# Moving the conv branch product of a hybrid streaming-encoder block from behind the gates to between attention and the gates

## The chip, the cores and the metric

The kernel runs on one core of a Trainium2 chip. The metric is the device time of one execution in microseconds (us), and less is better. The engines are named as in the profile: PE (TensorE, matrix products), DVE (VectorE), ACT (ScalarE), POOL (GpSimd) and SP (SyncE, which here issues every DMA between the core's memory, SBUF, and the chip's main memory, in one queue, in order). Every engine runs its own instructions in order, and waits at an instruction until what it needs is there.

## The reference

One layer for a sequence of 1024 rows of 1024 numbers, in float32. Cut to what matters here:

```python
h = modulate(rms_norm(x, g_pre_mix), sh1, sc1)
proj = h @ w_in                      # -> bg, cg, u, q, k, v (512 each), ga, gb (1024 each)
y_conv = short_conv_branch(bg, cg, u, conv_w) @ w_proj_conv     # bg * conv3(cg * u), 512 -> 1024
o = stick_breaking_attention(q, k, v)                           # 8 heads of 64
y_attn = o @ w_proj_attn                                        # 512 -> 1024
merged = sigmoid(ga) * y_conv + sigmoid(gb) * y_attn
x = x + gt1 * rms_norm(merged @ w_out, g_post_mix)
h2 = modulate(rms_norm(x, g_pre_mlp), sh2, sc2)
x = x + gt2 * rms_norm(square(relu(h2 @ w_mlp_in)) @ w_mlp_out, g_post_mlp)
```

`mod = c @ w_ada + b_ada` gives `sh1` to `gt2`, six rows of 1024.

## The kernel before, in words

Every large product is made of three products of reduced-precision parts: each operand is split into a high part (an ACT cast) and a low part (a DVE subtraction of the high part), and PE adds high x high, high x low and low x high in a PSUM bank of 128x512 (there are 8 banks). Activations lie transposed, channels on the 128 partitions. `hT` (`hTh`, `hTl`) holds `h` in both parts.

The stages, in order of time in the program:

1. Norm, first modulation, `hT`, and the value rows of attention.
2. Attention, with PE's order written out by hand. Between its steps PE does the other projections of `h` (q, k, and bg, cg, u of the conv branch) as `fill`, in banks `mm` (L545). The conv branch's four products `y` (128x1024 each, tile `cy`) are stored in `y_d` (L627) as they are done. Some 86 projection matmuls are left when attention ends.
3. The gates, `proj[:, 3072:]` for `ga` and `gb`, 2048 columns in 8 pairs of 128. Each pair is one Strassen-Winograd product: 7 products in place of 8, in the order 1, 2, 6, 5, 7, 3, 4, each of 4 x 3 matmuls (L233). Its right factors come from `hT` and are the same for all pairs: 1, 2 and 3 are parts of `hT`, and 4 to 7 are made from sums of its quarters: DVE adds high and low parts again (`e`, 16 additions L93), makes 16 differences (L90), and ACT and DVE split 16 results into `gy4`, `gy6`, `gy7` and, in place, a part of `hT` (factor 5). Its left factors are 128x512 sums of `w_in` columns, split for each pair (tiles `t`). `done` evicts a result: a DVE sum (L843), the sigmoid on ACT (L844) and a store to `sg_d` (L846). Between the factors runs `modulation`: four products of `c` with a 1024-column part of `w_ada`, each as 8 multiply-adds on DVE (L144) into `acc`, over 8 loads of 512 KB into two buffers; `acc` is first cleared by POOL (L139), gets a part of `b_ada` by DMA (L140), and PE sums its partitions at the end (L865 in rounds 1 and 4, L153 in 2 and 3).
4. The conv branch: `y` is loaded from `y_d` (`yr`), split (`br`), and multiplied with `w_proj_conv`: 8 rows of 128 channels, 2 halves, 12 matmuls each, 192 in all. DVE multiplies each bank with the gate row loaded from `sg_d` (L951).
5. The attention branch, the same with `o` from `o_d` (`or`) and `w_proj_attn`: DVE multiplies with the gate (L976), adds the conv row (L93), and splits the sum into `mT` (`mTh`, `mTl`).
6. `mix_block`: `w_out`, the norm and the residual; then the MLP's two products.

Inside stages 1 and 2 the order on PE is the hand-written one. Elsewhere a scheduler orders the instructions of each engine by its own estimate of their times. Tiles come from pools: a tile that is opened where another pool lay waits until the old tiles there have been read.

Of the kernel before, what the change touches and what calls it, by code (L numbers as in the profile page):

```python
# [8 lines left out]
F32 = mybir.dt.float32  # L9
# [7 lines left out]
P = 128  # L17
# [13 lines left out]
def block_kernel(  # L31
# [40 lines left out]
    y_d = dram.tile([4, P, T], F32, name="y_d")  # L72
# [464 lines left out]
    psm = open_pool(psm_es, "psm", bufs=3, space=PSUM)  # L537
# [13 lines left out]
    with ExitStack() as es:  # L551
# [235 lines left out]


    ga0 = 3 * CW + 3 * NH * HD
    psg_es = ExitStack()  # L790
    with ExitStack() as es:
        gt = open_pool(es, "gt")
        gy = open_pool(es, "gy", side="right")
        yop = resident(hT)
# [3 lines left out]
        quads = []  # L798
        for k in range(4):
            q11, q12, q22, q21 = (gt.tile([P, HALF], F32, tag="e", name=nm("e"), bufs=8) for _ in range(4))  # L800
            quads.append([[q11, q12], [q21, q22]])
            for o, i in zip((q11, q12, q22, q21), (1, 5, 3, 2)):
                hi, lo = yop[i][k]
                add(o, f(hi), f(lo), nc.vector)
            for o, l, r in ((q11, q12, q11), (q12, q22, q12), (q22, q22, q11), (q21, q21, q22)):
                sub(o, l, r, nc.vector)
            for i in (6, 7, 4):
                split_t(quads, yop, i, k)
        for _ in fill:
            pass  # L810
        for k in range(4):
            split_t(quads, yop, 5, k)
        psm_es.close()
        psg = open_pool(psg_es, "psg", bufs=8, space=PSUM)

        MODS = (14, 2)
        calls = [0]

        def gate_factors(p):
            split_of = pair_factors(  # L820
                column_pair(w_in, ga0 + 2 * p * P),
                lambda: gt.tile([P, 4, P], F32, tag="s", name=nm("s"), bufs=4),
                lambda i: gt.tile([P, 4, P], F32R, tag="e", name=nm("t"), bufs=8)
                if p >= 2 and i in (7, 3, 4)
                else gt.tile([P, 4, P], F32R, tag="t", name=nm("t"), bufs=12),
            )
# [8 lines left out]
            return with_modulation  # L835

        def gate_products(p, xop):
            fo = out_pair()

            def done(r, half, ps, kept):  # L840
                o = fo[r][:, half, :]
                if kept is not None:
                    nc.vector.tensor_tensor(o, ps, kept, op=ALU.add)  # L843
                nc.scalar.activation(o, ps if kept is None else o, AF.Sigmoid)  # L844
                if (r, half) in ((0, 1), (1, 0)):
                    nc.sync.dma_start(sg_d[2 * p + r], flat(fo[r]))  # L846

            if p == KC - 1:
                for _ in mods:
                    pass  # L850
                load_y()
            return pair_products(psg, 4, xop, yop, keeper(fo), done)
# [27 lines left out]
        yq = []  # L880

        def load_y():
            for k, tag in zip(range(4), ("cu", "cy", "acc", "row")):
                t = cv.tile([P, T], F32, tag=tag, name=nm("yr"), bufs=1)
                nc.sync.dma_start(t, y_d[k])
                yq.append(t)

        pipeline(KC, gate_factors, gate_products)
# [4 lines left out]
    gp_es, br_es, cy_es = ExitStack(), ExitStack(), ExitStack()  # L893
    gp = open_pool(gp_es, "gp", bufs=16)
    ow = open_pool(br_es, "ow")
    cyp = open_pool(cy_es, "cyp", side="right")
# [4 lines left out]
    def branch_operand(pool, raw, engines):  # L901

        parts_of = []
        for k in range(4):
            hi, lo = (pool.tile([P, T], F32R, name=nm("br")) for _ in "hl")
            split(raw[k], hi, lo, engines[k])
            parts_of.append([(hi[:, h], lo[:, h]) for h in halves])
        return parts_of

    def branch_weight(w, p, eng):  # L910

        raw = raw_tile((P, 4, 2 * P))
        nc.sync.dma_start(
            raw, w[:, 2 * p * P : (2 * p + 2) * P].rearrange("(a p) n -> p a n", p=P)
        )
        hi, lo = raw_tile((P, 4, 2 * P), "wh"), raw_tile((P, 4, 2 * P), "wl")
        hi, lo = hi.bitcast(F32R), lo.bitcast(F32R)
        split(raw, hi, lo, eng)
        return hi, lo

    def branch(w, operand, m0, use, engines):

        ahead = branch_weight(w, 0, engines[0])
        for p in range(KC // 2):
            hi, lo = ahead
            if p + 1 < KC // 2:
                ahead = branch_weight(w, p + 1, engines[p + 1])
            for m in (2 * p, 2 * p + 1):
                sg = ow.tile([P, T], F32, tag="sg", name=nm("sg"), bufs=4)
                nc.sync.dma_start(sg, sg_d[m0 + m])  # L930
                s = slice((m % 2) * P, (m % 2 + 1) * P)
                for half in range(2):
                    ps = bank(psg, "s")
                    mm3(ps, [((hi[:, k, s], lo[:, k, s]), operand[k][half]) for k in range(4)])
                    use(m, half, ps, sg[:, halves[half]])


    OPERANDS = "vvvv vvvv vvvv vvvv"
    MERGED = "vvvvvvvvvvvvvvvv vvvvvvvvvvvvvvvv"
    branch_on, merged_on = on(OPERANDS), on(MERGED)  # L940
    yop = branch_operand(cyp, yq, branch_on[0])
    oq = []
    for k, tag in zip(range(4), ("cu", "cy", "acc", "row")):
        t = cv.tile([P, T], F32, tag=tag, name=nm("or"), bufs=1)
        nc.sync.dma_start(t, o_d[k])
        oq.append(t)
# [8 lines left out]
    cy_es.close()  # L955
# [17 lines left out]

    def merged(m, half, ps, sg):
        o, t = ow.tile([P, HALF], F32, tag="o", name=nm("o"), bufs=4), g1[m, half]
        nc.vector.tensor_tensor(o, ps, sg, op=ALU.mult)  # L976
# [15 lines left out]
    branch(w_proj_attn, oop, KC, merged, branch_on[3])  # L992
# [388 lines left out]
```

## Time and profile before

| | us |
|---|---|
| median of 3 runs | 1456.64 |
| lowest and highest | 1454.67, 1458.77 |
| the profiled execution | 1457.99 |
| its span in the profile | 1456.3 |

The profiled execution is 1.35 us longer than the median of the runs, and its time is 1.7 us longer than the span, which goes from the first to the last instruction. An engine's busy time is a share of the span; where PE, the busiest engine, waits, and for whom, is read from the views of the trace.

### The profile page before, as it was taken

The page shows a single profiled execution, that of the slowest core. Times are in us where ns is not written, and L with a number is a line of the kernel's source. Part 1 is how long each engine was busy: PE and PEld are TensorE (multiplying, and loading weights), DVE is VectorE, ACT ScalarE, POOL GpSimd, SP SyncE. Part 2 cuts the span into 40 slices and gives each one's busy share as a digit, 9 for nine tenths or more (in the row PEclk, how much of TensorE's full clock was granted, in tenths as well). Part 3 has the DMA queues.
Part 4 walks back from the last instruction along what each step waited for, and adds up shares of the span by engine and source line. Part 5 has one row for each costly group of instructions (what it writes and reads, how often), then busy time and mean ns, then how long its engine had stood idle before and what let it go on. Part 6 is the DMA issues. An engine that isn't in the chain of part 4 may idle for free.

```text
span 1456.3 us, 17855 instructions
## 1 busy us (share of the span) xinstructions
PE 1374.5 (94%) x6281; PEld 1123.7 (77%) x6281; DVE 1076.1 (74%) x1684; ACT 645.2 (44%) x1301; POOL 95.8 (7%) x187
## 2 busy tenths in 40 slices
PE   5899899999996999899999899999999899999996
PEld 4788777887884888678878688888888688888884
DVE  6728888887879777357635886665654998989998
ACT  5636656565533433333346643333322544434432
POOL 1002112212200000000011000000000000000001
PEclk9899999999998999999999899999999999999999
DMA  8501110111114567575432243322346425151224
GB/s 299 179 15 35 36 53 21 37 37 51 44 55 129 190 222 236 202 250 167 136 103 100 73 145 116 117 87 89 116 142 217 152 80 174 59 165 38 77 84 173
DMA packets 107566, 171.09 MB, mean 117 GB/s; under 512 B 7322, under 2 KB 66766, under 8 KB 107476
## 3 DMA queue, kind: packets, MB, share of 16 engines
q1 hardware_dynamic: 107476, 169.95, 35.5%
q8 instruction: 49, 0.80, 0.2%
q14 instruction: 41, 0.34, 0.1%
HBM read 132.16 MB, written 37.76 MB: 117 GB/s over the span
## 4 chain that ended last, share of the span: by engine, by line
PE 76%; DVE 14%; DMA 3%; ACT 3%; issue 3%; POOL 1%; SPq 0%; DVEq 0%; ACTq 0%; POOLq 0%
PE s L233 28%; PE s L1274 19%; PE mm L545 8%; PE s L120 4%; PE s L121 4%; PE s L122 4%; PE v L507 3%; DVE pt L688 2%; PE o L729 2%; DVE a L692 2%; PE tr L718 1%; DMA wa<-in_w_ada_dram 1%; DMA raw<-in_w_in_dram 1%; POOL a L684 1%; DVE tu L90 1%
## 5 line engine op out<-in xcount | busy, mean ns | idle before, releaser
L1274 PE MATMUL s<-y,y 128*128 128x512 f32 x984 | 236.8, 393 | 8.4 <-DVE ffacc L1284 3.9
L1274 PEld LDWEIGHTS s<-y,y 128*128 128x128 f32 x984 | 185.4, 189 | 50.5 <-DVE ffacc L1284 5.1
L545 PE MATMUL mm<-hTh,wh 128*128 128x512 f32 x320 | 129.1, 403 | 0.0
L545 PE MATMUL mm<-hTl,wh 128*128 128x512 f32 x320 | 125.5, 392 | 0.0
L545 PE MATMUL mm<-hTh,wl 128*128 128x512 f32 x320 | 125.5, 392 | 0.0
L103 ACT CAST y<-g 128x512 fp32r<-128x512 f32 x104 | 58.6, 620 | 128.0 <-PE s L1274 107.6
L233 PE MATMUL s<-hTh,t 128*128 128x512 f32 x256 | 83.9, 398 | 14.4 <-ACT hTh L103 14.3
L688 DVE TENSOR_TENSOR_SCAN pt<-pt,dmask 128x128 f32<-128x128 f32 (+3 forms) x64 | 87.1, 1365 | 8.5 <-ACT pt L681 8.1
L1284 DVE TENSOR_TENSOR ffacc<-s,ffacc 128x512 f32<-128x512 f32 x124 | 83.7, 691 | 8.9 <-PE s L1274 8.8
L233 PE MATMUL s<-mTh,g 128*128 128x512 f32 x256 | 86.2, 404 | 3.7 <-ACT mTh L103 3.7
L103 ACT CAST tu<-tr 128x512 fp32r<-128x512 f32 (+2 forms) x112 | 49.1, 439 | 78.2 <-PE tr L718 49.5
L131 POOL TENSOR_TENSOR rstd<-var,mhalf 128x1 f32<-128x1 f32 x32 | 23.1, 725 | 920.0 <-DVE var L128 919.9
L90 DVE TENSOR_TENSOR tu<-tr,tu 128x512 fp32r<-128x512 f32 (+2 forms) x112 | 55.1, 494 | 34.5 <-ACT tu L103 33.5
L233 PE MATMUL s<-mTh,h 128*128 128x512 f32 x240 | 79.6, 396 | 0.0
L1274 PE MATMUL s<-fr,fr 128*128 128x512 f32 x288 | 74.6, 392 | 0.0
L233 PE MATMUL s<-y,g 128*128 128x512 f32 x288 | 71.5, 391 | 0.0
L233 PE MATMUL s<-y,h 128*128 128x512 f32 x288 | 71.5, 391 | 0.0
L90 DVE TENSOR_TENSOR y<-g,y 128x512 fp32r<-128x512 f32 x104 | 67.9, 691 | 3.8 <-PE s L1274 2.0
L545 PEld LDWEIGHTS mm<-hTh,wl 128*128 128x128 f32 x320 | 60.2, 188 | 13.4
L233 PEld LDWEIGHTS s<-hTh,t 128*128 128x128 f32 x256 | 48.6, 190 | 25.9 <-ACT hTh L103 14.6
L545 PEld LDWEIGHTS mm<-hTl,wh 128*128 128x128 f32 x320 | 60.5, 189 | 8.9
L545 PEld LDWEIGHTS mm<-hTh,wh 128*128 128x128 f32 x320 | 60.4, 189 | 8.8
(258 smaller groups left out, 3138.3 us busy)
## 6 DMA issues: line engine op xcount, KB each, us to landing
raw<-in_w_in_dram SPq DMA_DIRECT2D x38, 512.0 KB, 3.8
wa<-in_w_ada_dram SPq DMA_DIRECT2D x32, 512.0 KB, 3.9
raw<-in_w_mlp_in_dram SPq DMA_DIRECT2D x32, 512.0 KB, 3.8
g<-in_w_mlp_out_dram SPq DMA_DIRECT2D x40, 256.0 KB, 3.7
g<-f_d SPq DMA_DIRECT2D x40, 256.0 KB, 3.5
sg<-sg_d SPq DMA_DIRECT2D x16, 512.0 KB, 3.5
f_d<-wl SPq DMA_DIRECT2D x16, 512.0 KB, 5.0
f_d<-wh SPq DMA_DIRECT2D x16, 512.0 KB, 2.6
```

What stands on the lines that cost most here:

```text
L90: eng.tensor_tensor(o, a, b, op=ALU.subtract)
L103: nc.scalar.copy(hi, src)
L120: nc.tensor.matmul(ps, lh, rh, start=i == 0, stop=False)
L121: nc.tensor.matmul(ps, lh, rl, start=False, stop=False)
L122: nc.tensor.matmul(ps, ll, rh, start=False, stop=i == n - 1)
L233: nc.tensor.matmul(ps, l, r, start=first and k == 0 and j == 0, stop=k == nk - 1 and j == 2, skip_group_check=True,)
L507: nc.tensor.matmul(vb[b], l, r, start=k == 0 and i == 0, stop=k == KC - 1 and i == 2, skip_group_check=True,)
L545: nc.tensor.matmul(ps, w[a][:, k, :], hT[b][:, k, s], start=k == 0 and i == 0, stop=k == KC - 1 and i == 2, skip_group_check=True,)
L688: nc.vector.tensor_tensor_scan(pt[:, 0:w][:, ::-1], pt[:, 0:w][:, ::-1], dmask[:, T - w : T][:, ::-1], 1.0, ALU.mult, ALU.max,)
L692: nc.vector.tensor_tensor(a[:, 0:w], a[:, 0:w], pt[:, 1 : w + 1], op=ALU.mult)
L1274: nc.tensor.matmul(ps, l[:, s], r, start=start and j == 0 and n == 0, stop=j == len(fs) - 1 and n == 2, skip_group_check=True,)
L1284: nc.vector.tensor_tensor(o, ps, o, op=ALU.add)
```

## The change

The conv branch product (stage 4) is taken from behind the gates and put between the last projection and the gates. `y` 0 to 2 are loaded back from `y_d`; `y` 3 is taken from SBUF. The result of the product, without a gate, goes by ACT copies (`rows`) to memory, `yc_d`. While it runs, the right factors of the gates are made in turns with it: `right_factors` is a generator with one step per DVE instruction or split, of which one is taken at every fourth projection step (`FILL_TURNS`) and two after each bank of the conv branch (`BANK_TURNS`). In this stretch the order on PE, DVE and ACT is the order of the code (`manual_schedule`). The first two left factors of the first gate pair are made in the same stretch, in weight buffers. When a conv row's gate is done, DVE multiplies it with the row loaded from `yc_d`, and `sg_d` holds the gated conv row. The attention branch then loads both: the other gate as before, and the gated conv rows as 16 halves. Stage 4 as such is gone; the operand of the attention branch is loaded where `load_y` stood (`load_o`).

The diff, cut to its core:

```diff
-    y_d = dram.tile([4, P, T], F32, name="y_d")
+    y_d = dram.tile([3, P, T], F32, name="y_d")
+    yc_d = dram.tile([KC, P, T], F32, name="yc_d")
...
-                nc.sync.dma_start(y_d[k, :, s], y[:, s])
+                if k < 3:
+                    nc.sync.dma_start(y_d[k, :, s], y[:, s])
...
+        def right_factors():
+            quads = []
+            for k in range(4):
+                q11, q12, q22, q21 = (eslot() for _ in range(4))
+                quads.append([[q11, q12], [q21, q22]])
+                for o, i in zip((q11, q12, q22, q21), (1, 5, 3, 2)):
+                    hi, lo = yop[i][k]
+                    add(o, f(hi), f(lo), nc.vector)
+                    yield
+                for o, l, r in ((q11, q12, q11), (q12, q22, q12), (q22, q22, q11), (q21, q21, q22)):
+                    sub(o, l, r, nc.vector)
+                    yield
+                for i in (6, 7, 4):
+                    split_t(quads, yop, i, k)
+                    yield
+                if k:
+                    split_t(quads, yop, 5, k - 1)
+                    yield
+            split_t(quads, yop, 5, 3)
+            yield
+
+        def conv_branch(raws, turns):
...
+            for n, _ in enumerate(fill):
+                if n in LEAD:
+                    what, k = LEAD[n]
+                    {"y": operand, "w": weight}[what](k)
+                elif n % 4 in FILL_TURNS:
+                    next(turns)
+            yield
+            weight(1)
+            operand(3)
...
+            banks = [(m, half) for m in range(KC) for half in range(2)]
+            held = {}
+            for n, (m, half) in enumerate(banks[:4] + banks):
...
+                ks = range(3) if n < 4 else range(3, 4) if n < 8 else range(4)
...
+                if n >= 4:
...
+                    nc.scalar.copy(rows[m][:, halves[half]], ps)
+                    if half:
+                        nc.sync.dma_start(yc_d[m], rows[m])
+                if n >= 4 and m % 2 == 0 and half == 0 and p + 2 < KC // 2:
+                    weight(p + 2)
+                if n == 17:
+                    gate_split.append(gate_factors(0))
+                    for i in (1, 2):
+                        gate_first[i] = gate_split[0](i)
+                for _ in range(BANK_TURNS):
+                    next(turns, None)
+            for _ in turns:
+                pass
...
+        LEAD = {1: ("y", 0), 3: ("y", 1), 5: ("y", 2), 18: ("w", 0)}
+        FILL_TURNS, BANK_TURNS = (0,), 2
...
+        with tc.manual_schedule(
+            engines={mybir.EngineType.PE, mybir.EngineType.DVE, mybir.EngineType.Activation}
+        ):
+            stages = conv_branch(raws, right_factors())
...
         def gate_products(p, xop):
             fo = out_pair()
+            yc = {}
+            if p < KC // 2:
+                for r in range(2):
+                    for half in range(2):
+                        yc[r, half] = eslot()
+                        nc.sync.dma_start(yc[r, half], yc_d[2 * p + r, :, halves[half]])
...
                 nc.scalar.activation(o, ps if kept is None else o, AF.Sigmoid)
+                if yc:
+                    nc.vector.tensor_tensor(o, o, yc[r, half], op=ALU.mult)
...
-        pipeline(KC, gate_factors, gate_products)
+        gt = open_pool(es, "gt")
+        pipeline(KC, gate_factors, gate_products, first=(gate_first, gate_split[0]))
...
-    yop = branch_operand(cyp, yq, branch_on[0])
...
-    def gated(m, half, ps, sg):
-        t = g1[m, half] = gslot()
-        nc.vector.tensor_tensor(t, ps, sg, op=ALU.mult)
-
-    branch(w_proj_conv, yop, 0, gated, branch_on[1])
-    oop = branch_operand(ow, oq, branch_on[2])
+    oop = branch_operand(oq, lambda: ow.tile([P, T], F32R, name=nm("br")), branch_on[2])
...
+    def gate_rows(m):
+        sg = ow.tile([P, T], F32, tag="sg", name=nm("sg"), bufs=4)
+        nc.sync.dma_start(sg, sg_d[KC + m])
+        for half in range(2):
+            t = g1[m, half] = gslot()
+            nc.sync.dma_start(t, sg_d[m, :, halves[half]])
+        return sg
```

What the change does to the instructions of an engine is seen in three places. In these rows the number behind a name is that of the buffer. The first place is PE at the end of the projections (`mm` banks). Before:

```order
L545 MATMUL mm_4093<-hTh,wh_3906 128x512
L545 MATMUL mm_4093<-hTl,wh_3906 128x512
L545 MATMUL mm_4093<-hTh,wl_3907 128x512
L233 MATMUL s_4174<-hTh,t_4136 128x512
L233 MATMUL s_4174<-hTl,t_4136 128x512
L233 MATMUL s_4174<-hTh,t_4137 128x512
```

In the changed kernel (`br`: the parts of `y`; `wh`, `wl`: the parts of `w_proj_conv`):

```order
L546 MATMUL mm_4060<-hTh,wh_3907 128x512
L546 MATMUL mm_4060<-hTl,wh_3907 128x512
L546 MATMUL mm_4060<-hTh,wl_3908 128x512
L903 MATMUL s_4102<-br_3963,wh_4042 128x512
L903 MATMUL s_4102<-br_3964,wh_4042 128x512
L903 MATMUL s_4102<-br_3963,wl_4043 128x512
```

The first product of the gates, on the whole right factor in `hT`, stood behind the projections; now the 192 matmuls of the conv branch stand there, and the gates behind them. PE has 6247 matmuls in both programs.

The second place is DVE where the gates begin. In the changed kernel (`s`: sums of left factors, `t`: their parts, `acc`: the modulation's sum):

```order
L91 TENSOR_TENSOR gy4l<-e_4313,gy4h 128x512
L94 TENSOR_TENSOR s_4437<-raw_4381,raw_4383 128x512
L91 TENSOR_TENSOR s_4438<-s_4437,raw_4381 128x512
L91 TENSOR_TENSOR s_4439<-raw_4381 128x512
L91 TENSOR_TENSOR hTl<-e_4194,hTh 128x512
L145 SCALAR_TENSOR_TENSOR acc_4651<-wa_4654,vcols,acc_4651 128x1024
L91 TENSOR_TENSOR s_4440<-raw_4383,s_4438 128x512
L91 TENSOR_TENSOR hTl<-e_4310,hTh 128x512
L91 TENSOR_TENSOR t_4446<-s_4438,t_4445 128x512
L91 TENSOR_TENSOR t_4450<-s_4437,t_4449 128x512
L91 TENSOR_TENSOR t_4454<-s_4439,t_4453 128x512
```

Before, the same sums of the first pair stood among the quads and the conv taps:

```order
L90 TENSOR_TENSOR s_4147<-raw_4134,s_4145 128x512
L90 TENSOR_TENSOR t_4153<-s_4145,t_4152 128x512
L90 TENSOR_TENSOR e_3942<-e_3942,e_3940 128x512
L90 TENSOR_TENSOR t_4157<-s_4144,t_4156 128x512
L90 TENSOR_TENSOR e_3960<-e_3960,e_3958 128x512
L90 TENSOR_TENSOR gy7l<-e_3941,gy7h 128x512
L90 TENSOR_TENSOR hTl<-e_3940,hTh 128x512
```

The quads (`e`, `gy`, `hTl`) are now nearly done where the sums `s` of the first pair begin, and a modulation step stands between the sums and `t_4446`, the low part of the left factor of product 6. The first `s` tile lies where the parts of `y` lay, and waits for PE's last reading of them.

The third place is ACT at the end of the gates. Before (`yr`: `y` loaded back):

```order
L103 CAST wh_5451<-raw_5449 128x1024
L313 COPY wl_5259<-s_5276 128x512
L844 ACTIVATE wl_5259<-wl_5259 128x512
L844 ACTIVATE wl_5259<-s_5276 128x512
L103 CAST br_5425<-yr_5268 128x1024
```

In the changed kernel (`or`: `o` loaded):

```order
L104 CAST wh_5788<-raw_5786 128x1024
L314 COPY wl_5600<-s_5617 128x512
L989 ACTIVATE wl_5600<-wl_5600 128x512
L989 ACTIVATE wl_5600<-s_5617 128x512
L104 CAST br_5764<-or_5609 128x1024
```

The order is the same, the tiles are not: the `br` tiles of the attention branch lie where `hTl` lies, so the cast waits for the last gate matmul that reads `hTl`, the last but one of the gates. The `br` tiles of the conv branch lay on the other side, at the place of `gy`.

## Rows read from the trace of the kernel before

**Rows 1.** Part 1 of the page: busy time of each engine, its share of the span, and instructions.

```profile
PE 1374.5 (94%) x6281; PEld 1123.7 (77%) x6281; DVE 1076.1 (74%) x1684; ACT 645.2 (44%) x1301; POOL 95.8 (7%) x187
```

**Rows 2.** Who PE waited for: us in total, times, longest. The first row is of the whole run and the longest there; the next three are all that there are from 475 to 622 us, the last is the only one from 622 to 720.

```profile
PE s L233 <- ACT hTh L103: 14.3, 1, 14.3
...
PE s L865 <- DVE acc L144: 2.1, 1, 2.1
PE s L233 <- ACT wl L313: 1.6, 2, 1.0
PE s L233 <- ACT wh L313: 1.5, 1, 1.5
...
PE s L120 <- ACT wh L103: 1.0, 1, 1.0
```

**Rows 3.** PE's timeline around the end of the projections: start, us, engine, line, operation, out<-in, count, and in brackets the idle time before and its releaser. Between the second and the third row four rows with six matmuls are left out.

```profile
436.51 0.39 PE L545 MATMUL mm<-hTh,wl 128*128 128x512 f32 x1
451.15 0.76 PE L233 MATMUL s<-hTh,t 128*128 128x512 f32 x1 [14.25 <-ACT hTh L103]
...
454.27 0.40 PE L233 MATMUL s<-hTl,t 128*128 128x512 f32 x1
454.51 0.63 PE L233 MATMUL s<-hTh,t 128*128 128x512 f32 x2
```

**Rows 4.** Stretches: from:to, length, busy time of PE, PEld, DVE, ACT and POOL with their instructions, PE's granted clock as a share of full speed, the DMA engines' busy share, and GB/s.

```profile
440.00:450.00 10.00, 0.00 (x0) 0.00 (x0) 10.00 (x18) 1.24 (x2) 0.00 (x0) 0.53 0.25 79
450.00:455.00 5.00, 3.85 (x11) 3.05 (x12) 5.00 (x9) 1.78 (x3) 0.00 (x0) 0.57 0.32 87
455.00:460.00 5.00, 5.00 (x23) 4.12 (x22) 5.00 (x9) 3.94 (x7) 0.00 (x0) 1.00 0.25 80
```

**Rows 5.** The chain of work that ended last, from 475 to 622 us: start, us, what.

```profile
532.73 1.68 PE s L153 x16
...
594.56 1.98 PE s L865 x4
596.54 16.38 PE s L233 x72
...
619.32 0.91 PE s L120 x4
```

**Rows 6.** DVE's timeline, columns as in rows 3.

```profile
418.46 4.91 DVE L93 TENSOR_TENSOR e<-hTh,hTl 128x512 f32<-128x512 f32 x8
...
446.70 0.69 DVE L90 TENSOR_TENSOR s<-raw 128x512 f32<-128x512 f32 x1
447.30 0.70 DVE L93 TENSOR_TENSOR e<-hTh,hTl 128x512 f32<-128x512 f32 x1
...
464.73 1.31 DVE L90 TENSOR_TENSOR gy4l<-e,gy4h 128x512 fp32r<-128x512 f32 x2
```

**Rows 7.** The instructions that read `yr`: count, shortest, median and longest ns, and the first and last start in us.

```profile
L103 ACT CAST br<-yr x4: 1039/1054/1061, 617.1 to 620.0; 128x1024 fp32r<-128x1024 f32 x4
L90 DVE TENSOR_TENSOR br<-yr,br x4: 1217/1220/1226, 618.2 to 622.2; 128x1024 fp32r<-128x1024 f32 x4
```

**Rows 8.** Groups of ACT's instructions from 440 to 625 us: busy us, mean ns of one, idle time before and its releasers.

```profile
L103 ACT CAST t<-raw 128x512 fp32r<-128x512 f32 x22 | 13.5, 616 | 27.4 <-PE s L233 15.6 <-DMA raw<-in_w_in_dram 10.7 <-issue 1.2
L313 ACT COPY wh<-s 128x512 f32<-128x512 f32 x16 | 9.3, 581 | 3.0 <-issue 1.7 <-PE s L233 1.4
```

**Rows 9.** The timeline of all engines from 504 to 510 us, where the second modulation begins.

```profile
504.19 0.95 POOL L139 MEMSET acc<- 128x1024 f32 x1 [103.92 <-PE s L865]
...
505.17 0.24 SPq L140 DMA_DIRECT2D acc<-in_b_ada_dram  x1
...
507.47 2.61 DVE L144 SCALAR_TENSOR_TENSOR acc<-wa,vcols,acc 128x1024 f32<-128x1024 f32 x2 [3.17 <-DMA acc<-in_b_ada_dram]
```

**Rows 10.** Part 6 of the page: issues of a DMA, KB each, median us from issue to landing.

```profile
f_d<-wh SPq DMA_DIRECT2D x16, 512.0 KB, 2.6
```

**Rows 11.** The same from 400 to 720 us.

```profile
sg_d<-wl SPq DMA_DIRECT2D x8, 512.0 KB, 5.9
sg_d<-wh SPq DMA_DIRECT2D x8, 512.0 KB, 7.0
```

**Rows 12.** A group of DVE's instructions from 610 to 720 us, columns as in rows 8.

```profile
L951 DVE TENSOR_TENSOR g<-s,sg 128x512 f32<-128x512 f32 x16 | 10.8, 689 | 17.1 <-PE s L122 17.1
```

**Rows 13.** Three more stretches, columns as in rows 4.

```profile
622.00:633.00 11.00, 10.04 (x45) 7.87 (x43) 7.25 (x9) 3.94 (x4) 0.00 (x0) 1.00 0.99 360
633.00:707.40 74.40, 74.38 (x329) 61.31 (x328) 49.58 (x71) 21.16 (x31) 0.00 (x0) 1.00 0.51 165
475.00:530.00 55.00, 55.00 (x240) 44.83 (x240) 40.24 (x56) 25.04 (x45) 0.95 (x1) 1.00 0.65 218
```

**Rows 14.** PE's column sums of the second and third modulation (columns as in rows 7).

```profile
L153 PE MATMUL s<-ones,acc x32: 169/250/250, 532.6 to 563.6; 128*128 128x1 f32 x32
```

**Rows 15.** The loads of `w_ada` in the gates (tile `wa`).

```profile
DMA to landing us min/median/max: 3.6/3.9/7.2
```

More of the change, by code (lines that the diff above doesn't have):

```diff
@@ L536, in block_kernel @@
     psm_es = ExitStack()
[L537 removed]
+    psm = open_pool(psm_es, "psm", bufs=3, space=PSUM, side="right")
     def project(ps, w, half):
@@ L786, in block_kernel, with branch_operand, branch_weight, branch @@
     attn.close()
+    def branch_operand(raw, new, engines):
+        parts_of = []
+        for k in range(4):
+            hi, lo = new(), new()
+            split(raw[k], hi, lo, engines[k])
+            parts_of.append([(hi[:, h], lo[:, h]) for h in halves])
+        return parts_of
+    def branch_weight(w, p, eng=nc.vector):
+        raw = raw_tile((P, 4, 2 * P))
+        nc.sync.dma_start(
+            raw, w[:, 2 * p * P : (2 * p + 2) * P].rearrange("(a p) n -> p a n", p=P)
+        )
+        hi, lo = raw_tile((P, 4, 2 * P), "wh"), raw_tile((P, 4, 2 * P), "wl")
+        hi, lo = hi.bitcast(F32R), lo.bitcast(F32R)
+        split(raw, hi, lo, eng)
+        return hi, lo
+    def branch(w, operand, begin, use, engines):
+        ahead = branch_weight(w, 0, engines[0])
+        for p in range(KC // 2):
+            hi, lo = ahead
+            if p + 1 < KC // 2:
+                ahead = branch_weight(w, p + 1, engines[p + 1])
+            for m in (2 * p, 2 * p + 1):
+                at = begin(m)
+                s = slice((m % 2) * P, (m % 2 + 1) * P)
+                for half in range(2):
+                    ps = bank(psg, "s")
+                    mm3(ps, [((hi[:, k, s], lo[:, k, s]), operand[k][half]) for k in range(4)])
+                    use(m, half, ps, at)
+    OPERANDS = "vvvv vvvv vvvv vvvv"
+    branch_on = on(OPERANDS)
     ga0 = 3 * CW + 3 * NH * HD
@@ L809, in block_kernel, with eslot @@
[L809 to L814, printed above, removed]
+        def eslot(dtype=F32, shape=(P, HALF)):
+            return ge.tile(list(shape), dtype, tag="e", name=nm("e"), bufs=8)
+        def right_factors():
+            quads = []
+            for k in range(4):
+                q11, q12, q22, q21 = (eslot() for _ in range(4))
[15 more added lines that the diff above has]
+            yield
@@ new lines, in conv_branch, with operand, weight @@
+        def conv_branch(raws, turns):
+            new = lambda: bo.tile([P, T], F32R, name=nm("br"))
+            parts_of = {}
+            def operand(k):
+                hi, lo = new(), new()
+                split(raws[k], hi, lo)
+                parts_of[k] = [(hi[:, h], lo[:, h]) for h in halves]
+            def weight(p):
+                weights[p] = branch_weight(w_proj_conv, p)
+            weights = {}
+            for n, _ in enumerate(fill):
[7 more added lines that the diff above has]
+            operand(3)
+            rows = {}
+            banks = [(m, half) for m in range(KC) for half in range(2)]
+            held = {}
+            for n, (m, half) in enumerate(banks[:4] + banks):
+                p, s = m // 2, slice((m % 2) * P, (m % 2 + 1) * P)
+                hi, lo = weights[p]
+                ks = range(3) if n < 4 else range(3, 4) if n < 8 else range(4)
+                if n < 4:
+                    held[m, half] = bank(psg, "s")
+                ps = held.pop((m, half)) if 4 <= n < 8 else held[m, half] if n < 4 else bank(psg, "s")
+                for k in ks:
+                    yh, yl = parts_of[k][half]
+                    for i, (l, r) in enumerate(((hi, yh), (hi, yl), (lo, yh))):
+                        nc.tensor.matmul(
+                            ps, l[:, k, s], r, start=k == 0 and i == 0, stop=k == 3 and i == 2,
+                            skip_group_check=True,
+                        )
+                if n >= 4:
+                    if m not in rows:
+                        rows[m] = cv.tile(
+                            [P, T], F32, tag=("acc", "row", "cu")[m % 3], name=nm("yr"), bufs=1
+                        )
+                    nc.scalar.copy(rows[m][:, halves[half]], ps)
[11 more added lines that the diff above has]
+                pass
@@ L910, in branch_weight @@
[L910 to L935, printed above, removed]
@@ L991, in block_kernel @@
     late = []
-    branch(w_proj_attn, oop, KC, merged, branch_on[3])
+    branch(w_proj_attn, oop, gate_rows, merged, branch_on[3])
     merge()
```

71 lines of the change are left out of this document (33 added, 38 removed).

## The prediction

> **What bounds the kernel now.** Start with the page: PE is busy for 94% of 1456.3 us [rows 1], so time is lost where PE stands still, and the view to read next is who PE waited for. One wait leads it by far: 14.3 us, once, for ACT's `hTh` [rows 2]. The timeline of PE shows the place: the last projection matmul (L545) starts at 436.51, and the first gate product (L233) at 451.15, after 14.25 us of nothing [rows 3]. The windows show two things there: DVE is busy for all of 440 to 450 while PE does nothing, and PE's granted clock falls to 0.53 and is 0.57 in 450 to 455, that is, partly at the 1.2 GHz level, before it is 1.00 again (2.4 GHz) [rows 4]. In that dip eight matmuls start from 451.15 to 454.27, and the ninth at 454.51 [rows 3]: 3.36 us, where eight at the full clock take 8 x 0.2275 = 1.82 (72 matmuls in 16.38 us [rows 5]). The dip costs 1.54 us.
>
> What is DVE doing? It begins the right factors (`e`, 128x512) at 418.46 and makes the last `gy4l` at 464.73; its instructions follow each other every 0.60 us, 0.69 to 0.70 us each [rows 6]. So the end of the wait is a DVE chain through four quads, with gate factors, taps and the start of the modulation mixed in. Meanwhile 192 matmuls of the conv branch, which need none of this, stand behind the gates.
>
> **What the change moves.** *The gap.* PE's order puts the conv branch's 192 matmuls straight behind the last projection: 192 x 0.2275 = 43.7 us, from 436.9 to 480.6. They need `y`: products 0 to 2 are loaded back and split while the last projections run (three ACT casts of 1.05 us and three DVE subtractions of 1.22 [rows 7], which stand where eight `e` additions, 4.91 us, stood [rows 6]; the conv taps behind them start at about 423.3 in place of 423.4, no cost). Product 3 is split from SBUF at about 440, and is read first after 36 matmuls, at 445.1. Evictions: 16 ACT copies at 0.58 (as L313 [rows 8]), one per 2.73 us of PE, over eight banks. I see no PE wait here.
>
> Does DVE finish the right factors by 480.6? Between 440 and 481 it has some 40 instructions of 0.60 us and three of 1.2, about 28 us of work, but the hand-set orders tie it to ACT, and ACT to PE's banks. Walked by hand: the weights of the fourth pair of rows are split at 461 (their buffer is read until 458.7), the casts of the first two gate factors (0.62 each [rows 8]) stand behind the eviction of the bank that ends at 475.1, so their low parts are ready at 477.5; PE wants them at 480.6: 3.1 us to spare. So the whole 14.25 and the 1.54 go: **-15.8**. If that cover were gone, PE would wait for what exceeds the 3.1.
>
> *Gate entry.* Here something is late next. Products 1 and 2 of the first pair give PE work until 480.6 + 24 x 0.2275 = 486.1, and four matmuls more, until 487.0; then it needs `t_4446`. On DVE that stands behind `s_4437` (which waits until the conv operand in the same memory has been read, 478.5), and behind the first modulation sum. That sum needs `acc`: the row copied at 475.7 is stored from there, POOL clears the buffer (0.95), the bias comes in (issued 505.17, used 507.47 in the trace: 2.3 [rows 9]). SP issues that store behind three loads of conv rows, which wait for DVE's `gy` splits until 468.8, so these are not late. A 512 KB store lands after 2.6 [rows 10] to 7.0 us [rows 11]: the sum can start at 482.7 (DVE free) to 486.0. Then 1.2 + 3 x 0.60 + 0.1: `t_4446` at 485.8 to 489.1, a wait of 0 to 2.1, with two more low parts of that pair queued behind it. I take **+0.5**, near the low end, since few other transfers are in flight then. The Trainium skill (DMA: Bandwidth & Descriptors, Anatomy of one DMA) counts about 2.0 us plus the bytes at 436 GB/s for a DMA that GpSimd issues, and warns that the receipt of a write to HBM can be slow. As an estimate that is 3.2 us for this store, and by it the term is zero and the time 0.5 lower; the trace's 5.9 to 7.0 for `sg_d` stores go the other way.
>
> *Gates.* The same 672 products. DVE gets 16 multiplications there (L991 of the changed kernel) for the 16 that leave the branch (L951, 0.69 [rows 12]): 11 us more work in a stage where it is busy 40.24 of 55.00 us [rows 13]. They stand behind the sigmoid and ahead of a store, and no product waits for them: 0; if DVE had no room, 0.60 each. The stage's own waits are those behind the fourth modulation: 2.1 + 1.6 + 1.5 = 5.2 us [rows 2]. From PE's last column matmul before it (563.6 [rows 14]) to its first one (594.56 [rows 5]) are 31.0 us, in which PE has 113 products, 25.7 us. In the changed order 112 products stand there, 25.5: **+0.3**. Bounds: -5.2 if the chain keeps ahead, +4 if its loads land at the 7.2 us maximum of [rows 15] more often. The third has 132 products where 123 sufficed from 532.73 on [rows 5] without a wait; the first two have 170 and 168.
>
> *Gates to attention branch.* Before, the first cast of the branch operand (from `yr`) is at 617.1 [rows 7], ahead of the last gate product, because its tiles lie elsewhere. Now the operand's tiles lie where `hTl` lies, and ACT's cast waits for PE's last but one product. PE then waits about 1.05 - 0.23 + 0.1 = 0.9 us, does four matmuls (0.9), and waits 0.3 for DVE's 1.22. **+1.2**; bounds 0.8 and 1.05 + 1.22 = 2.3. The old wait of 1.0 for the second weights [rows 2] stays.
>
> *Attention branch.* PE and DVE have what they had there. Transfers are denser (a rival below): 0. The order of the first MLP pairs shifts a little; PE had no wait in them: 0.
>
> **Sum.** -15.8 + 0.5 + 0.3 + 1.2 = -13.8. The profiled execution: 1456.3 - 13.8 = 1442.5 of span, 1.7 around it, 1444.2, against its 1457.99. The median of the runs is 1456.64, 1.35 below that execution, so I say **1442.8 us**.
>
> **Rivals.** *Less comes through.* The gate entry at its upper bound (2.1), the modulation at +4, the cover of 3.1 us overrun by a few: a gain of 5 to 10, some 1449. For it speaks that DVE runs in a fixed order behind ACT and POOL; against, that each piece has to go wrong by its bound.
>
> *More comes through.* The modulations now begin in a stage with more products behind them (170 and 168 per round); if all stay ahead, the 5.2 go too: 1437.6. Against: 112 products (25.5 us) still stand before the last.
>
> *The change does not do it.* DVE is merely moved: if ACT's evictions hold it back by as much as it gains, PE stands at 480.6 for as long as before, and the time stays near 1456.6. Against: 28 us of DVE work in 43.7.
>
> *Slower: transfers bound the attention branch.* Its place: all gate rows, 16 loads of 0.262 MB (gated conv rows) and 8 of 0.524 (the other gate), one late store and the first five `w_out` rows: 4.2 + 4.2 + 0.5 + 2.6 = 11.5 MB, now in 43.7 us, 263 GB/s, where the two branches together ran at 165 [rows 13]. At 165 the branch takes 69.7 us, 26.0 more: 1456.64 - 13.8 + 26.0 = 1468.8. It decides below 11.5 MB in 43.7 + 13.8 = 57.5 us, 200 GB/s. Against: the 11 us from 622 moved 360 GB/s [rows 13], and 165 was demand. The Trainium skill (DMA: Bandwidth & Descriptors, Specifications) puts the limit of HBM for one core at about 358 GB/s, which that row agrees with, so by it the branch can be fed.
>
> **Chances.** Forecast (1440 to 1447) 0.60; more 0.12; less 0.15; no effect 0.07; slower 0.06. The range 1438.0 to 1450.5 holds the forecast, nearly all of "more" and four fifths of "less", about 0.82. Faster by over 0.3% (4.4 us, about what a measurement of this kernel can tell) is the first three: 0.87; same 0.07; slower 0.06.
>
> **What would show it.** After the last projection matmul PE goes on with the conv branch (L903 of the changed kernel) within 0.1 us, at clock 1.00 through 430 to 480; the first L234 starts near 480.6; a wait of 0 to 2.1 us for DVE's `t` near 487; four column rounds of L1012 and L154, the last with a wait of about 5 for `acc`; a wait of 0.9 and 0.3 for `br` at the gates' end, near 648 (480.6 + 0.5 + the 168.2 from 451.15 to 619.32 [rows 3, 5] less 1.54, + 0.3); then no PE wait for `sg` or `g`. Wrong would be: PE waiting for `wl` or `wh` of the gate factors near 480, any modulation round but the last holding PE by over 3 us, or `s` banks held by DVE waits for `sg_d` loads after 650.

## The result, and the profile after

| | before | after |
|---|---|---|
| median, us | 1456.26 (4 runs) | 1447.38 (4 runs) |
| lowest and highest | 1454.67, 1458.77 | 1446.19, 1447.72 |
| span of the profiled execution | 1456.3 | 1446.0 |

The ratio is 0.9936, with a 95% interval of 0.9919 to 0.9953. The same kernel measured a second time, beside other runs of the kernel before (E6 below), gave 0.9906, 0.9886 to 0.9926. So the change makes the kernel faster, by about 9 us in the first measurement and 14 in the second. The forecast was 13.8 and 1442.8 us, the range 1438.0 to 1450.5; as a ratio to 1456.64 that is 0.9905, outside the first interval and in the middle of the second.

Part 1 of the page of the changed kernel answers to [rows 1]: PE's work is the same (both traces have 6281 matmuls, where 6247 is said above), and the span is shorter.

```profile
PE 1375.6 (95%) x6281; PEld 1124.2 (78%) x6281; DVE 1075.1 (74%) x1684; ACT 653.0 (45%) x1317; POOL 95.3 (7%) x187
```

Who PE waited for, from 437 to 720 us, answers to [rows 2]. The 14.3 us for `hTh` are gone. In their place there is nothing, but the waits of the gate stage are still there, on other lines.

```profile
PE s L234 <- ACT wh L314: 2.1, 1, 2.1
PE s L234 <- DVE wl L988: 1.8, 1, 1.8
PE s L1012 <- DVE acc L145: 1.2, 1, 1.2
PE s L121 <- ACT wh L104: 1.0, 1, 1.0
PE s L121 <- ACT br L104: 0.9, 1, 0.9
PE s L234 <- ACT wl L314: 0.7, 1, 0.7
```

PE's timeline (columns as in [rows 3]) at five places: the end of the projections, the first gate product, the first use of `t_4446`, and the two longest waits.

```profile
436.95 0.39 PE L546 MATMUL mm<-hTh,wl 128*128 128x512 f32 x1
437.18 0.62 PE L903 MATMUL s<-br,wh 128*128 128x512 f32 x2
...
480.69 0.39 PE L234 MATMUL s<-hTh,wh 128*128 128x512 f32 x1
...
486.81 0.39 PE L234 MATMUL s<-gy6l,t 128*128 128x512 f32 x1
487.20 0.73 PE L234 MATMUL s<-gy6h,t 128*128 128x512 f32 x2
...
586.49 0.50 PE L234 MATMUL s<-hTh,e 128*128 128x512 f32 x1 [1.80 <-DVE wl L988]
...
588.83 1.05 PE L234 MATMUL s<-hTh,e 128*128 128x512 f32 x2
...
617.44 0.50 PE L234 MATMUL s<-gy7h,e 128*128 128x512 f32 x1 [2.08 <-ACT wh L314]
...
618.70 1.05 PE L234 MATMUL s<-gy7h,e 128*128 128x512 f32 x2
```

The conv branch follows the last projection matmul after 0.23 us, which is the ordinary pitch, and the first gate product starts at 480.69. The forecast said 480.6. Behind each of the two waits, a pair of matmuls takes 1.05 us where a pair takes 0.62 elsewhere: PE is at half its clock again. The stretches of the trace (columns as in [rows 4]) show the granted clock:

```profile
440.00:450.00 10.00, 10.00 (x46) 8.29 (x45) 6.26 (x10) 2.84 (x5) 0.00 (x0) 1.00 0.35 107
585.00:590.00 5.00, 3.51 (x11) 2.87 (x12) 5.00 (x8) 2.26 (x4) 0.00 (x0) 0.80 0.58 197
615.00:620.00 5.00, 2.92 (x11) 2.06 (x10) 3.73 (x5) 1.10 (x2) 0.00 (x0) 0.87 0.86 321
620.00:625.00 5.00, 3.79 (x10) 1.93 (x9) 2.49 (x3) 1.68 (x3) 0.00 (x0) 0.79 0.92 334
651.00:694.00 43.00, 41.39 (x179) 33.30 (x180) 36.55 (x55) 17.96 (x28) 0.00 (x0) 1.00 0.79 281
660.00:665.00 5.00, 4.03 (x19) 3.01 (x18) 3.80 (x7) 1.57 (x2) 0.00 (x0) 1.00 1.04 412
```

From 440 to 450, where before PE did nothing at 0.53 [rows 4], it is busy all the time at 1.00. Instead, the clock falls around 590 and around 620. Before, it stayed at 1.00 behind the waits of this stage; the longest of them ended at 594.56:

```profile
592.00:600.00 8.00, 5.91 (x23) 3.90 (x22) 2.58 (x3) 3.15 (x6) 0.00 (x0) 1.00 0.65 231
```

**Where the time went.** What comes before the gates' stretch ended up to 3 us earlier or later from one execution to the next, with the same code too (the conv branch began at 437.18 in the first profile of the changed kernel and at 434.14 in the second, and between these in the six others that have it there). So spans are not compared. The stretches below are read from PE's timeline and begin where the projections end (before: 451.15 less the wait of 14.25).

| stretch, us | before | after | E6, after again | forecast |
|---|---|---|---|---|
| projections to first gate product | 14.25 | 43.51 | 43.52 | 43.7 |
| gates, to the first matmul of a branch behind them | 168.01 | 170.74 | 167.92 | 168.2 |
| branches behind the gates, to the first matmul of the mix | 88.68 | 45.74 | 45.97 | 45.3 |
| sum | 270.94 | 259.99 | 257.41 | 257.2 |
| against before | | -10.95 | -13.53 | -13.7 |

(Forecast: for the gates 168.01 + 0.5 + 0.3 + 0.9 - 1.54, since 0.9 of the transition falls before that first matmul; for the branch 88.68 less 192 x 0.2275, with the other 0.3.) The gates are what differs between the first profile and the forecast, by 2.5 us, and the second profile has them where the forecast put them, though not by the forecast's reasons (below).

### The profile page after: what moved, and what is told of

Same layout as the page of the kernel before. It is cut to its first block, busy times and chain, and to the rows that moved or that the text cites. A ratio compares the mean times of both kernels' runs of the same rounds, so it can differ in the third digit from the quotient of the medians.

```text
span 1446.0 us, 17935 instructions
## 1 busy us (share of the span) xinstructions
PE 1375.6 (95%) x6281; PEld 1124.2 (78%) x6281; DVE 1075.1 (74%) x1684; ACT 653.0 (45%) x1317; POOL 95.3 (7%) x187
## 4 chain that ended last, share of the span: by engine, by line
PE 69%; DVE 14%; DMA 7%; issue 4%; ACT 3%; POOL 1%; SPq 0%; DVEq 0%; ACTq 0%; POOLq 0%
PE s L234 24%; PE s L1379 19%; PE mm L546 10%; PE v L508 3%; PE s L903 3%; DVE pt L690 2%; PE s L123 2%; PE s L121 2%; PE s L122 2%; DMA wa<-in_w_ada_dram 2%; PE o L731 2%; DVE a L694 2%; PE tr L720 1%; DVE acc L145 1%; DMA raw<-in_w_in_dram 1%
## 5 line engine op out<-in xcount | busy, mean ns | idle before, releaser
L234 PE MATMUL s<-hTh,t 128*128 128x512 f32 x208 | 67.5, 394 | 0.0
L731 PE MATMUL o<-tu,vs 128*128 128x256 f32 x320 | 57.0, 297 | 9.6 <-DVE ot L741 5.0
```

What stands on the lines that cost most here:

```text
L234: nc.tensor.matmul(ps, l, r, start=first and k == 0 and j == 0, stop=k == nk - 1 and j == 2, skip_group_check=True,)
L731: nc.tensor.matmul(po[:, : 2 * P], v, part[:, 0:5:4, :] if j and jp == g else part[:, 2 * j + 1 : 2 * j + 3, :], start=jp == 0 and j == 0 ...
```

## The experiments

Eight kernels were run. Their order here is that of the questions; ratios are to the kernel before, run on the same chip.

**E6. The changed kernel again**, with no edit.

> The changed kernel once more, unaltered, to see whether the waits behind the third and fourth modulation and the two clock dips come again. If the waits are the change's and the dips follow them: waits of 1.8, 2.1 and 1.2 us within 0.3 each, two dips of about 1.5 us, and a ratio to the kernel before of 0.993 to 0.995. If the dips are a matter of the single execution: the same waits, with none or one dip, and a span shorter by 1.5 to 3 us.

Measured: 1443.19 us, ratio 0.9906 (0.9886 to 0.9926). Who PE waited for in the gates, and PE's timeline at the longest of these waits:

```profile
PE s L234 <- ACT wh L314: 3.5, 1, 3.5
...
PE s L234 <- ACT wl L314: 0.7, 1, 0.7
PE s L1012 <- DVE acc L145: 0.5, 1, 0.5
```

```profile
612.16 0.80 PE L234 MATMUL s<-gy7h,e 128*128 128x512 f32 x1 [3.49 <-ACT wh L314]
612.75 0.63 PE L234 MATMUL s<-gy7l,e 128*128 128x512 f32 x1
```

So neither expectation held as it stood. The wait in the third round (1.8 at 586) did not come, those of the fourth did, with other sizes, and there was one dip (seven matmuls in 3.15 us, from 612.16 to 615.31). The gates' waits are 5.8 us in one profile and 4.6 in the other; whether the third round holds PE, and how often the clock drops, differs from execution to execution.

**E1. A third buffer for the modulation.**

```diff
-                    [P, T + 2 * (k % 2)], F32, tag=("cy", "cu")[k % 2], name=nm("wa"), bufs=1
+                    [P, T + 2 * (k % 3 == 1)], F32, tag=("cy", "cu", "row")[k % 3], name=nm("wa"), bufs=1
```

The reading behind it comes from three views of the changed kernel. DVE's timeline (columns as in [rows 6]):

```profile
583.95 1.28 DVE L145 SCALAR_TENSOR_TENSOR acc<-wa,vcols,acc 128x1024 f32<-128x1024 f32 x1 [1.17 <-DMA wa<-in_w_ada_dram]
...
585.75 0.69 DVE L988 TENSOR_TENSOR wl<-s,wl 128x512 f32<-128x512 f32 x1
...
614.36 1.28 DVE L145 SCALAR_TENSOR_TENSOR acc<-wa,vcols,acc 128x1024 f32<-128x1024 f32 x1 [1.41 <-DMA wa<-in_w_ada_dram]
615.56 0.68 DVE L988 TENSOR_TENSOR wh<-s,wh 128x512 f32<-128x512 f32 x1
...
621.75 1.28 DVE L145 SCALAR_TENSOR_TENSOR acc<-wa,vcols,acc 128x1024 f32<-128x1024 f32 x1 [2.52 <-DMA wa<-in_w_ada_dram]
```

and ACT's:

```profile
616.28 0.63 ACT L989 ACTIVATE wh<-wh 128x512 f32<-128x512 f32 x1 [5.22 <-DVE wh L988]
616.82 0.57 ACT L314 COPY wh<-s 128x512 f32<-128x512 f32 x1
```

Read backwards from PE's wait until 617.44: ACT's copy that frees the bank (L314) stands behind the sigmoid (L989), which waits for DVE's eviction (L988), and that stands behind a multiply-add of the modulation (L145), which waits for its load. PE's rows blame ACT; the cause is two engines behind it. The Trainium skill (TensorE: Matmul & The Clock Gate, Architectural detail) says that ACT and DVE take their instructions strictly in order; these rows agree. The load waits for its buffer: the one that the multiply-add at 583.95 needed was issued at 579.80, right after the multiply-add that ran from 578.49 to 579.77.

> The changed kernel, with a third buffer for the loads of w_ada in the modulation (the tile that holds the modulation's row). Theory A: the waits of PE in the gates (1.80 at 586, 2.08 at 617, 1.21 at 623 us) come from DVE, which stands at a multiply-add of the modulation for its load, with evictions and left factors queued behind it; two buffers let only two loads be under way. With three, these 5.1 us of waits go, and the two clock dips behind the first two of them (8 matmuls each, about 1.5 us each) go with them: 8.2 us less, span near 1437.8, time near 1439. Theory B: DVE is simply too busy since it got the sixteen multiplications with the conv rows: the waits stay, 1447. Theory C: the loads are bound by the transfer rate, so a third one only takes longer: the waits stay, 1447. If the dips have a cause of their own, 1442.

Measured: 1436.55 us, ratio 0.9858 (0.9837 to 0.9879). Who PE waited for, from 430 to 720 us; no wait for the modulation is left:

```profile
PE s L1172 <- DVE wh L1162: 1.0, 1, 1.0
PE s L121 <- ACT wh L104: 1.0, 1, 1.0
PE s L121 <- ACT br L104: 0.9, 1, 0.9
PE s L234 <- ACT wl L314: 0.7, 1, 0.7
```

The gates took 161.53 us, 9.2 less than in the first profile of the changed kernel and 6.4 less than in the second, and the granted clock of the stretch from 478 to 639 was 1.00. DVE's waits for `wa` fell from 12.3 to 3.8 us. PE's order in the gates is that of the changed kernel: in both traces 170, 166, 124 and 104 matmuls of the gates stand before the four column sums of the modulation. So the waits and the dips came from these loads and their two buffers (A); DVE was not too busy (B), and the transfers were not at their limit (C). The 0.7 at the end of the gates stays, so it is not the modulation's.

**E2. The kernel before, with the same third buffer.**

> The kernel before, with the same third buffer. Theory A: its waits of 2.1, 1.5 and 1.0 us behind the fourth modulation go, the later one of 0.7 and the 14.3 us gap stay: 4.5 us less, 1451.8. It had no clock dip behind these waits, so nothing more comes back. Theories B and C: B says nothing of this kernel beyond its smaller DVE load, C says no change, 1456.3.

Measured: 1454.82 us, ratio 0.9974 (0.9964 to 0.9984). Who PE waited for, from 430 to 720 us:

```profile
PE s L233 <- ACT hTh L103: 14.2, 1, 14.2
...
PE s L233 <- ACT wl L313: 0.7, 1, 0.7
```

The gates took 162.54 us in place of 168.01, that is 5.5 less, and the three waits of [rows 2] are gone. The stall belongs to the kernel before as much as to the changed one. The change only kept it.

**E8. The modulation four left factors earlier**, with two buffers.

```diff
-        MODS = (14, 2)
+        MODS = (10, 2)
```

> The changed kernel with the modulation begun four left factors earlier, the buffers as they are. Theory A (the pace of two buffers is slower than the pace of the left factors that the steps are tied to): the waits stay, 3 to 6 us in all, at the third and fourth round, 1444 to 1449. Rival (the last round has only too few products behind it): with an earlier start the waits go to 1 us or less, 1438 to 1440.

Measured: 1449.55 us, ratio 0.9944 (0.9926 to 0.9963). Who PE waited for in the gates:

```profile
PE s L1012 <- DVE acc L145: 5.2, 1, 5.2
...
PE s L234 <- ACT wh L314: 1.7, 1, 1.7
PE s L234 <- DVE wl L988: 1.1, 1, 1.1
```

With an earlier start the waits stay, and with 8.7 us (the 0.7 at the end among them) they are longer than theory A had them. But the run does not separate the two theories. The scheduler placed the column sums anew: 168, 132, 143 and 97 matmuls stand before the four, so the last round has fewer behind it than the 104 of the changed kernel, and its 5.2 us fit the rival as well. The 1.7 are of another kind: ACT's copy waits for the store of a gate row out of `wh` (573.33 to 576.97). What decides is E1, where the same matmuls stand before each sum and only the pace of the loads is another.

**E3. The changed kernel without the multiplications in the gates.**

```diff
-            if p < KC // 2:
+            if False:
                 for r in range(2):
                     for half in range(2):
                         yc[r, half] = eslot()
```

> The changed kernel without the loads of the conv rows and the sixteen multiplications in the gates (the conv rows are left out of the gates, so the output lacks the conv branch). Theory A: DVE still waits for the loads of w_ada; waits of PE of 3 to 5 us stay behind the third and fourth modulation, 1443 to 1447. Theory B: with 11 us of DVE work and 4.2 MB of loads gone the waits go: 1439.

Measured: 1443.74 us, ratio 0.9902 (0.9881 to 0.9922). In the gates PE still waits for the modulation:

```profile
PE s L234 <- ACT wh L314: 3.1, 1, 3.1
```

From the projections to the mix it took 257.03 us; the changed kernel took 257.41 and 259.99. The 11 us of DVE work and the 4.2 MB thus cost nothing that stands out from the changed kernel's own spread. The comparison is not a clean one: without them the scheduler placed the column sums elsewhere (216, 121, 119 and 108 matmuls stand before them).

**E5. PE's order alone set by hand.** DVE and ACT are left to the scheduler in the conv branch.

```diff
         with tc.manual_schedule(
-            engines={mybir.EngineType.PE, mybir.EngineType.DVE, mybir.EngineType.Activation}
+            engines={mybir.EngineType.PE}
         ):
```

> The changed kernel, with only PE's order set by hand in the conv branch; DVE and ACT are ordered by the scheduler, which puts the right factors earlier, in runs. Theory 1 (the conv branch as cover is what counts, and any order that makes the factors within its 43.5 us will do): no wait of PE over 2 us between 437 and 490, time within 3 us of 1447.4. Theory 2 (the turns are needed): the parts of y and of w_proj_conv come late behind the factors, PE waits 5 us or more near 437, or for the first gate factors near 481, and the time is 1452 or more.

Measured: 1466.84 us, ratio 1.0056 (1.0037 to 1.0075): slower than before. Who PE waited for, and DVE's timeline where the longest wait ends:

```profile
PE s L903 <- DVE cy L627: 7.0, 2, 5.5
PE s L1012 <- DVE acc L145: 6.5, 1, 6.5
```

```profile
448.89 1.29 DVE L91 TENSOR_TENSOR e<-e,e 128x512 f32<-128x512 f32 x2
450.09 0.69 DVE L627 TENSOR_TENSOR cy<-mm,cy 128x512 f32<-128x512 f32 x1
```

The scheduler put the steps of the right factors ahead of the eviction that makes `y` 3. The conv branch, the cover, now waits for the work that it was to cover: 54.57 us in place of 43.5, with 7.4 us of waits and a granted clock of 0.67 from 450 to 460. The gates took 178.70, with 11.6 us of waits, most of them for the modulation; the last multiply-add alone waited 4.8 us for its load. Theory 2 holds, though at another place than it named: the fourth product of `y`, not its first parts.

**E7. No turns during the projections.** Eight steps of the right factors fall behind the conv branch.

```diff
-        FILL_TURNS, BANK_TURNS = (0,), 2
+        FILL_TURNS, BANK_TURNS = (), 2
```

> The changed kernel without the turns during the projections: the eight steps of the right factors that were made there (7 to 8 DVE instructions of 0.6 us) fall behind the conv branch, in among the first left factors and modulation steps. Theory 1 (the cover is nearly used up: the first gate factors are ready 3 us ahead, the last high parts of product 6 less than that): PE waits 4 to 8 us for gy6 or t near 488 and may dip in clock; the time is 4 to 9.5 us over the changed kernel, 1452 to 1457, as slow as before. Rival (the conv branch has cover to spare): no wait over 1 us, 1447.

Measured: 1441.65 us, ratio 0.9886 (0.9865 to 0.9906), not slower than the changed kernel in the same comparison (0.9906). Who PE waited for:

```profile
PE s L234 <- DVE t L91: 1.0, 1, 1.0
...
PE s L234 <- DVE gy6l L91: 0.7, 1, 0.7
...
PE s L234 <- ACT t L104: 0.5, 1, 0.5
```

The expectation missed. At the gate entry PE waits 2.2 us in three pieces, not 4 to 8, with no dip; the later waits of the gates are 1.9, 1.0 and 0.7, and the gates took 168.25, as in E6. Two things had been left out: the first multiply-add of the modulation started 1.3 us behind the first gate product (481.52) in place of 3.4 (484.06), since its bias was there when DVE came to it; and while the last `gy6l` was made (until 491.8), PE had matmuls on `hTh` and `hTl` between those on `gy6` in its order. Whether the turns during the projections gain anything can't be told from this; that the cover isn't as tight as 3 us, can. Here too the scheduler moved a column sum (the first stands behind 216 matmuls in place of 170), so the two kernels differ by more than the turns.

**E9. E1, with the mix's two loads of the modulation row ahead of the last rows of `w_out` and the rows of `x`.** The block that makes `g1r` moves up, ahead of `row_parts(3, ...)`:

```diff
+        g1r = [yslot(F32), yslot(F32)]
...
         row_parts(3, lambda: gslot(F32R))
         for k in range(4, KC):
             row_parts(k, yslot)
...
-        g1r = [yslot(F32), yslot(F32)]
```

> The changed kernel with the third buffer, and with the two loads of the modulation row for the mix (from mod_d) ahead of the last rows of w_out and the rows of x in the DMA queue. If the waits of 1.6 and 1.0 us at the first two blocks of the mix come from these loads, which end last there, PE waits 1 us or less in all there, and the time is 1.6 to 2.6 us less than with the third buffer alone, 1434 to 1435; if the rows of w_out are late in their place, the same time, 1436.5.

Measured: 1435.89 us, ratio 0.9851 (0.9833 to 0.9869), the same as E1. Who PE waited for at the mix:

```profile
PE s L1172 <- DVE wh L1162: 1.4, 1, 1.4
...
PE s L1172 <- ACT wh L1150: 0.8, 1, 0.8
```

2.2 us in place of E1's 2.6, where 1 or less was expected. In E1 DVE waited 4.2 us for these loads, in E9 it waits 4.2 us at its next step for ACT: the loads ended last there, but a chain just behind them ends almost as late.

All runs by the stretches of the table above, from the projections to the mix, in us:

| | to the gates | gates | branches | sum | ratio of the times |
|---|---|---|---|---|---|
| before | 14.25 | 168.01 | 88.68 | 270.94 | 1 |
| E2 before, third buffer | 14.25 | 162.54 | 88.61 | 265.40 | 0.9974 |
| after | 43.51 | 170.74 | 45.74 | 259.99 | 0.9936 |
| E6 after again | 43.52 | 167.92 | 45.97 | 257.41 | 0.9906 |
| E8 earlier modulation | 43.52 | 172.75 | 45.59 | 261.86 | 0.9944 |
| E5 PE's order alone | 54.57 | 178.70 | 45.32 | 278.59 | 1.0056 |
| E7 no turns in the projections | 43.52 | 168.25 | 45.33 | 257.10 | 0.9886 |
| E3 no multiplications | 43.52 | 168.24 | 45.27 | 257.03 | 0.9902 |
| E1 third buffer | 43.52 | 161.53 | 45.31 | 250.36 | 0.9858 |
| E9 E1, rows first | 43.52 | 161.54 | 45.33 | 250.39 | 0.9851 |

The sums agree with the ratios to within 0.2% of the time: 250.36 is 20.6 less than 270.94, 1.4% of 1456, and E1 measured 1.4%.

## Why the prediction was right, and where it was off

*The gap, -15.8.* Right. The 14.25 us and the dip behind them are gone, and the conv branch took 43.51 us without a wait. The forecast had the low parts of the first gate factors ready at 477.5, 3.1 us before their use; DVE made them from 476.59 to 477.9, and the first was wanted at 480.69. The clock was 1.00 throughout.

*Gate entry, +0.5.* Right in mechanism and size. The first multiply-add of the modulation, forecast for 482.7 to 486.0, started at 484.06, and `t_4446` was made from 486.46 to 487.15 (forecast 485.8 to 489.1). PE lost some 0.2 us at 487.2, so the lower term of zero is as near as the 0.5. The store behind it can be read, though: it was issued at 476.07, and POOL cleared the buffer at 480.97. These 4.9 us are more than the 3.2 that the prediction estimated from the Trainium skill (DMA: Bandwidth & Descriptors, Anatomy of one DMA), whose figure is for a DMA that GpSimd issues. The same store took 3.2 in E7 and 2.8 in E3, which leaves out the loads of the conv rows.

*The multiplications, 0.* Not contradicted: E3, without them, is within the spread of the changed kernel.

*The late modulation, +0.3.* Here the prediction was off, in its count and in its rule. It counted 132 matmuls ("products") before the third column sum of the changed kernel and 112 before the last; the traces have 124 and 104. These rows show PE's gate matmuls alone (from:to, length, busy PE and PEld, clock, DMA share, GB/s) between the last two sums, before and after:

```profile
564.00:594.50 30.50, 26.00 (x112) 20.51 (x111) 1.00 0.72 245
594.00:623.00 29.00, 25.56 (x104) 20.23 (x104) 0.94 0.76 244
```

By the prediction's own rule 104 matmuls, 23.7 us of the 31.0, leave 7.3 us of waiting, a term of about +2 and not +0.3; and in the third round, with 124 where 123 had sufficed, there is almost no margin. That round did hold PE for 1.8 us in the first profile and not in the second. The rule is too stiff as well: the 31.0 us (from PE's last column matmul to the first matmul of the last sum) were 29.0 and 29.8 in the two profiles of the changed kernel, 27.5 in E8 and 23.8 in E1. Their main part is the pace of the loads. With two buffers, a load of 4.3 us (the median after) and a multiply-add of 1.3 make a step in (4.3 + 1.3) / 2 = 2.8 us, an estimate; the eight steps of the last round took 21.9 us after, and 17.1 in E1 with three buffers. The waits of the gates' last rounds, with the 0.7 that no buffer removes, came to 5.8 and 4.6 us against 5.2, that is +0.5 and -0.6. That this is near the +0.3 is luck: a count too high and a chain taken too long cancel.

*The clock, missing.* The sum let the dip at 451 go and had no other, since [rows 2] holds three waits of 1.0 to 2.1 us there and the clock stayed at 1.00. After, two such waits brought one dip each: 19 matmuls from 586.49 to 592.53 took 6.04 us, where 19 at 0.2275 take 4.32, and 12 from 617.44, the last counted with its pitch of 0.43, took 4.24 for 2.73. Together 3.2 us, more than the 2.5 by which the gates missed the forecast (the dip of before, 1.54, is in that forecast already). In E6 there was one dip, and the sum came out at -13.53.

*Gates to attention branch, +1.2.* Right: 0.91 us for `br`, and four matmuls of `br`'s high parts that lead into one at 652.69 where 652.34 would be the pitch, 0.35 more.

*Attention branch and MLP, 0.* Nearly. PE itself waits for no `sg` or `g`. But the branch took 0.4 to 0.7 us more than forecast, and the chain of work of the changed kernel shows by which way:

```profile
656.36 8.07 DMA sg_d<-wh
...
665.09 1.06 ACT wh L104
666.20 0.50 PE s L121
```

The store of the last gate row takes 8.07 us where the median of these stores before was 7.0 [rows 11], and the next weights are cast into the memory that it reads. From the first matmul of the mix to the end of the span it took 748.4 us before and 748.8 after, within the 747.9 to 751.3 of all ten profiles (PE's waits at the mix were 3.3 us in place of 2.4).

*The rivals.* "Slower" fell: the stretch from 651 to 694 moved 281 GB/s, more than the 263 that it needed and far above the 200 at which it would decide, with up to 412 in 660 to 665. The prediction cited the Trainium skill (DMA: Bandwidth & Descriptors, Specifications) with a limit of 358 GB/s for one core; the 412 here, and the 360 of [rows 13], show that this is no ceiling for a core that runs alone, and the measurement decides. "No effect" fell with the row at 437.18. "More" didn't come with the change itself, since the stalls stayed; E1 and E2 show that some 4.5 of its 5.2 us were to be had by a buffer, and that the other 0.7 never belonged to the modulation. Its 1437.6 also lies just below the range that was said to hold nearly all of it. "Less" is near the first measurement, but by the clock and the third round; of the places named for it, only the modulation was one, and not by its bound of 4.

## What to carry to other kernels

Work that needs nothing from a slow chain is best put in front of that chain's first reader, but the cover is only as good as the order of the engine that makes both: E5 moved the same matmuls and ended 8 us slower than the kernel before, since DVE served the chain before the cover's own operand (11 us there; the rest is in the gates). When PE's waits name an eviction, follow the evicting engine back: here a multiply-add that waits for a load held evictions behind it, on DVE and through it on ACT, and a third buffer, one line, took 6 to 9 us more off the gates. Where a forecast counts what stands between two points of an engine's order, an edit elsewhere can move them: here 112 matmuls became 104. And a wait of 2 us may cost 3.5, as here where the clock fell behind one; a sum of such waits should carry that as a bound.

## What the hardware showed beside this

Whether a short wait of PE is followed by the lower clock differs from case to case. In the gates of these kernels eight waits were between 1.5 and 2.1 us long. Five were followed by matmuls at full pitch (1.51 and 2.09 before, 1.90 in E7, 1.71 in E8, 1.87 in E5), three by a dip (1.80 and 2.08 after, 1.94 in E5), and in these the half clock began only 1 to 3 us after PE had resumed. The waits of 3.1 us and more (E3, E6, 5.2 in E8, 6.5 in E5) each brought one. A dip after such a short wait cost 1.5 to 1.7 us, much as did the one behind the 14.25 us, and no row tells beforehand which wait will have one.
